# Where the operand tiles lie in SBUF: residues modulo 512 bytes in a float32r network on one core

## The chip, the cores and the metric

One core of a Trainium2 chip runs the whole program in one launch. The metric is the device time in microseconds; the median of three timed runs is 1638.51 us (1635.72, 1638.51, 1638.74). One more execution was taken with the hardware profiler, and all rows below come from it.

## The reference

A small network of 256 tokens and 1024 columns runs through ten stages, each of which adds to a residual x:

```
x = x + nsa_mixer(rms_norm(x), ...)          # sparse attention, 16 heads
x = x + swiglu(rms_norm(x), gate_up, down)   # feed forward, 2816 hidden columns
x = x + mla_mixer(rms_norm(x), ...)          # low-rank attention, 8 heads
x = x + swiglu(...)
# then, with norms before and after each part:
#   swiglu, convolution module, swiglu, swiglu, differential attention, swiglu

def swiglu(h, w_gate_up, w_down):
    gate, up = jnp.split(h @ w_gate_up, 2, axis=-1)
    return (jax.nn.silu(gate) * up) @ w_down
```

All is float32. Six of the stages are feed-forward stages of the same size; they are counted here from first to sixth.

## The kernel before

**Products.** A product of two float32 matrices is made of three float32r products, since each operand is split into a high and a low part that add up to it: low times high, high times low, high times high, into the same PSUM bank. That is `mm3` (L457 to L463), and its lines L460, L461 and L462 hold nearly all of TensorE's time. A float32r matmul has a stationary operand of 128 x 128, which TensorE loads first, and a moving operand of up to 512 columns.

**Weights.** They stream from HBM in units of 128 x 1024 (`wraw`, five buffers, SP's queue). ScalarE makes the high part (`whi`, L358, L361) and VectorE the low part (`wlo`, L359, L362), twelve buffers each. `pump` emits a piece of this work behind each product.

**A feed-forward stage** (`ffn`) multiplies x, transposed and split into `HTh` and `HTl` ([128, 2, 8, 128] each: token tile, chunk, token), by gate and up, and the hidden columns by the down weights. `ffn_order` lists its steps. There are three kinds of product:

- M, at the beginning and the end of a stage: `HT` (128 x 128) is stationary and 512 columns of weights move, into a bank `ps_g`. 192 products in a stage.
- W, in the long middle: 128 columns of weights are stationary, and both token tiles of `HT` move, as two pieces of 128 columns, 256 in all, into `ps_g`. 14 units of 48 products, 672 in a stage.
- D: the split hidden columns `hidTh` or `hidTl` (128 x 128) are stationary and 512 columns of the down weights move, into `ps_a`. 264 in a stage.

The middle is a loop of rounds: 48 W, then 12 D. The order of the instructions on TensorE is that of the program. The same kinds M and W occur in the other stages, with `HT`; the projections of the low-rank attention and the out-projection of the differential attention have other stationary operands (`ckh`, `qah`, `doTh` and their low parts) and 512 moving columns.

**Addresses.** Tiles lie in pools, and pools lie one behind the other; each tile takes its bytes per partition, rounded up to 32. Pools that are opened last (of a stage) lie last and are reused. So each address follows from the shapes of all tiles ahead of it. For the program before:

| tiles | address | modulo 512 |
|---|---|---|
| `c_g` (constants, 268 columns; holds `ident` and the gains) | 16512 | 128 |
| `ones` | 17600 | 192 |
| `x0`, `x1` | 18112, 22208 | 192 |
| `HTh`, `HTl` | 26304, 34496 | 192 |
| small pool (many tiles of some columns) | 45760 to 48895 | any |
| `wraw` x5, `whi` x12, `wlo` x12 | 48896 and on, 4096 each | 256 |
| first stage's pool for the first mixer: `c_nsa` (1 column) | 167680 | 256 |
| behind it `qT`, `kT0`, `kT1`, `V..` | 167712 and on | 288 |
| `hidTh`, `hidTl` of the 1st, 2nd, 4th and 6th feed-forward stage | 176896 and others | 256 |
| the same of the 3rd, behind `c_conv`, `hb` (16 columns), `z` | 191520 and on | 32 |
| the same of the 5th, behind `c_diff`, `lam` (4 columns), `gsub` (1) | 187712 and on | 320 |
| `doTh`, `doTl` of the differential attention | 190784, 198976 | 320 |
| `ckh`, `ckl`, `qah`, `qal` of the low-rank attention, behind `mgq` (1 column) | 192288 and on | 288 |

Of the kernel before, what the change touches and what calls it, by code (L numbers as in the profile page):

```python
# [8 lines left out]
F32 = mybir.dt.float32  # L9
# [6 lines left out]
T = 256  # L16
# [32 lines left out]
def ffn_order():  # L49
    """M: a quarter of the sums of 256 hidden columns (gate and up) of a token tile; W: gate or up of 128 hidden  # L50
    columns of both tiles, transposed; T: transpose what M made; D: 128 hidden columns into the down product;
    B: the transposes of a token tile; END: a token tile is done"""
    ops = []

    def m(t, g, hook=None):
        for q in range(4):
            if q == 2 and hook:
                ops.append(hook)
            ops.append(("M", t, g, q))

    def d(t, g, j=None):
        ops.extend(("D", t, g, i) for i in ((0, 1) if j is None else (j,)))

    m(0, 0)
    m(0, 1, ("T", 0, 0))
    d(0, 0, 0)
    ops.append(("T", 0, 1))
    d(0, 0, 1)
    d(0, 1, 0)
    ops.append(("B", 1))  # L70
    d(0, 1, 1)
    m(1, 0)
    m(1, 1, ("T", 1, 0))
    d(1, 0)
    ops.append(("T", 1, 1))
    ops.append(("W", 2, 0, 0))
    d(1, 1)
    ops.append(("W", 2, 0, 1))
    last = (2, 0)
    for g in range(2, NG - 2):  # L80
        for j in range(2):
            if (g, j) == (2, 0):
                continue
            ops.append(("W", g, j, 0))
            ops.append(("W", g, j, 1))
            d(0, *last)
            d(1, *last)
            last = (g, j)
    m(0, NG - 2)
    d(0, *last)  # L90
    d(1, *last)
    m(0, NG - 1, ("T", 0, NG - 2))
    d(0, NG - 2, 0)
    ops.append(("T", 0, NG - 1))
    d(0, NG - 2, 1)
    d(0, NG - 1)
    ops.append(("END", 0))
    m(1, NG - 2)
    m(1, NG - 1, ("T", 1, NG - 2))
    ops.append(("L", LEAD[0]))  # L100
    d(1, NG - 2, 0)
    ops.append(("T", 1, NG - 1))
    ops.append(("L", LEAD[1]))
    d(1, NG - 2, 1)
    d(1, NG - 1)
    ops.append(("END", 1))
    return ops


# ---------------------------------------------------------------- host layout  # L110
# [5 lines left out]
def lay_out(p):  # L116
    units, folds = [], {}

    def unit(a, gain=None):
        """gain: the norm gain that belongs to these rows, by name, the width of each part, and the column for each"""  # L120
        if gain:
            folds[len(units)] = gain
        a = np.ascontiguousarray(a.reshape(128, -1), dtype=np.float32)
        assert a.shape[1] <= UNIT
        units.append(a)
# [101 lines left out]
    for t in range(2):  # L227
# [5 lines left out]
        for h in range(16):  # L233
# [22 lines left out]
            ("g_sub", p["attn_subln_g_2"][0].reshape(128, 1)),  # L256
        ],
        "nsa": [
            ("live", live),
# [44 lines left out]
# ---------------------------------------------------------------- the program  # L304
class Weights:
    """The weights in the order in which they are used, each split into two float32r parts that add up to it."""
# [20 lines left out]
    def cut(self):  # L327
        """the pieces of the next unit, to be emitted one by one"""
# [22 lines left out]
    def drop(self):  # L351
        """the products with the oldest unit of the plain kind are done"""
        self.held.pop(0)
        self.refill()
# [11 lines left out]
    def room(self):  # L366
        """whether the unit that the next one takes the place of is used up"""
# [8 lines left out]
    def pump(self, n):  # L376
        """n columns of products are under way: convert a little of what comes next"""
# [27 lines left out]
class Net:  # L405
    def __init__(self, ctx, tc, io, index, widths, upto):
# [3 lines left out]
        self.small = ctx.enter_context(tc.tile_pool(name="small", bufs=3))  # L410
        self.psum = ctx.enter_context(tc.tile_pool(name="psum", bufs=1, space=bass.MemoryType.PSUM))
# [18 lines left out]
        self.nc.gpsimd.memset(self.ones, 1.0)  # L430
        self.HT = self.pair(self.main, [128, 2, 8, 128], "HT")
        self.warm(self.work(), WARM)

    def warm(self, ps, n):
        """n products that nothing uses, where the tensor engine would idle: its clock slows down if it does"""
# [29 lines left out]
    def rsqrt(self, ss, k, scale, eps, more=None, half=False, least=None, hold=True, soon=200):  # L465
        """(ss * scale + eps) ** -0.5, of k columns, halved if asked for; more: a second part of ss;
        least: 2 ** 26 eps, for each of the rows.
        Newton's steps from an estimate by the exponent, without their halves, which are put into the operand."""
# [25 lines left out]
    def split(self, hi, lo, src, scale=None):  # L494
        """hi + lo = src * scale"""
# [15 lines left out]
    def squares(self, src):  # L511
        """sums of squares along the free axis, one for each of the parts"""
# [12 lines left out]
    def ready(self, t):  # L525
        """x[t] is what the next stage starts with: start(t) transposes it into the operand of the products, and its norm
        comes after them; the gain of the norm is in the weights. norm[t]: 1 / rms, and 2 ** 26 1e-6 rms ** 2"""
# [24 lines left out]
    def preload(self, f, after):  # L552
        """the tables of a function, ahead of what needs them"""
# [3 lines left out]
    def spread(self):  # L557
        """1 / rms of all the tokens along the free axis, the same in every partition"""
# [12 lines left out]
    def lead(self, n):  # L571
        """n of the products of the first block of the next stage, for which the first token tile is ready"""
# [13 lines left out]
    def first(self):  # L586
        """the first block of a stage, and its weights"""
# [9 lines left out]
    # residual: x += scale * acc, or x += half * rms(acc) * gain  # L597
# [25 lines left out]
    # ------------------------------------------------------------ feed forward  # L623
    def ffn(self, ht, done, follow):
        nc = self.nc
        with ExitStack() as ctx:
# [11 lines left out]
            def gated(ps, t=None):  # L638
                """the gate's norm, with which the nonlinearity needs it; the other one's is left to the sums over the hidden columns"""
# [90 lines left out]
    def out_proj(self, t, oT, ws, acc=None, cs=range(8)):  # L730
        """oT [t] times a 1024 x 1024 weight, into two banks"""
# [12 lines left out]
    def own(self):  # L744
        """the next unit of the weights, and its number: out_proj marks it as used up"""
# [18 lines left out]
    # ------------------------------------------------------------ first mixer  # L764
# [5 lines left out]
    def nsa(self, ht, after):  # L770
# [3 lines left out]
        k = self.consts("nsa", keep)  # L774
        qT = keep.tile([128, 8, T], F32, name="qT", tag="qT")
        kT = [keep.tile([128, 4, T], F32, name=f"kT{b}", tag=f"kT{b}") for b in range(2)]
        V = [[keep.tile([128, 4, 64], F32, name=f"V{b}{t}", tag=f"V{b}{t}") for t in range(2)] for b in range(2)]
        gate = [keep.tile([128, 48], F32, name=f"gate{t}", tag=f"gate{t}") for t in range(2)]
        kcT = keep.tile([128, 4, 64], F32, name="kcT", tag="kcT")
        Vc = keep.tile([128, 64], F32, name="Vc", tag="Vc")  # L780
        gq = keep.tile([128, 1], F32, name="gq", tag="gq")
        inv = keep.tile([128, 2, 3], F32, name="inv", tag="inv")
# [9 lines left out]
        def operand(t):  # L792
            """x[t] as it is; its norm comes after the products"""
# [9 lines left out]
        def norms(t):  # L803
            """of the rows of x[t]: 1 / rms, half of it, and 1e-6 rms ** 2 as rsqrt takes it"""
# [42 lines left out]
        def compress(i, a):  # L847
            """a quarter of the products of both"""
# [79 lines left out]
        def block(name, t, i):  # L928
            """a quarter of a token tile times 512 columns"""
# [19 lines left out]
        gT = keep.tile([48, T], F32, name="gT", tag="gT")  # L949
# [173 lines left out]
    # ------------------------------------------------------------ second mixer  # L1123
    def tables(self, ctx):
        """the mask of the second mixer, and its rotations with the gains of its norms"""
# [10 lines left out]
    def mla(self, ht, after, tab):  # L1136
# [6 lines left out]
        gq = keep.tile([128, 1], F32, name="mgq", tag="mgq")  # L1143
# [4 lines left out]
        def rope(x, src, w, tmp):  # L1148
            """[128, n, 64]; the gains are in the tables"""
# [15 lines left out]
        # the norm of what is projected to a low rank comes after the products as well  # L1165
        rc, rc2, eq = ([self.small.tile([128, 1], F32, name=f"mv{i}{t}", tag=f"mv{i}{t}", bufs=1) for t in range(2)] for i in range(3))
# [110 lines left out]
        def attend(t, hb, bank):  # L1277
            """four heads; what it returns turns the weights, and then sums the values;
            the norm of the queries, positive, comes with the exponential"""
# [103 lines left out]
    # ------------------------------------------------------------ convolution  # L1383
    def conv_consts(self, ctx):
        pool = ctx.enter_context(self.tc.tile_pool(name="cc", bufs=1))
        k = self.consts("conv", pool)
        k["half"] = pool.tile([128, 16], F32, name="hb", tag="hb")
# [12 lines left out]
    def conv(self, k, bias_row, done):  # L1400
# [11 lines left out]
        def build(ch):  # L1412
            """four taps of 32 channels as a matrix, for each of the products of a chunk"""
# [34 lines left out]
        def spread(ch):  # L1448
            """32 channels at a time, beside themselves one, two and three tokens later"""
# [12 lines left out]
        def stats(ch, s, pc):  # L1462
            """shift is the mean of the first chunk"""
# [15 lines left out]
        def total(ch, s, sq):  # L1479
            """sums over the channels of (c - shift) and of its square"""  # L1480
# [11 lines left out]
        def weights(g, q):  # L1492
            """of 256 columns, a quarter; they have two uses"""
# [100 lines left out]
    # ------------------------------------------------------------ differential attention  # L1594
    def diff_consts(self, ctx):
# [3 lines left out]
        k["lam"] = lam = pool.tile([128, 4], F32, name="lam", tag="lam")  # L1599
# [4 lines left out]
        k["gs"] = pool.tile([128, 1], F32, name="gsub", tag="gsub")  # L1604
# [3 lines left out]
    def diff(self, k, done):  # L1608
# [113 lines left out]
        def do(kind, h, bank=None):  # L1722
            """the next step of head h; its products are followed by those of others until what they need is there"""
# [39 lines left out]
    def run(self):  # L1763
# [3 lines left out]
        def then(n, f, add=None):  # L1767
            """after a stage: the residual, and what the next stage starts with"""
# [70 lines left out]
```

## Time and profile before

| | |
|---|---|
| median of the timed runs | 1638.51 us |
| the profiled execution, first to last instruction | 1640.0 us |
| TensorE busy | 1609.4 us, 98% |
| VectorE, ScalarE busy | 1108.6 us (68%), 946.7 us (58%) |
| mean granted clock of TensorE, share of full speed | 0.992 |
| HBM read | 282.43 MB |
| W products (256 columns), whole run | 4608, recorded mean 280 to 282 ns |
| D products, whole run | 1584, recorded mean 392 to 396 ns |

A recorded duration of a matmul goes past the start of the next one, since matmuls are pipelined. What a product costs in a dense stretch is therefore read from start to start in the timeline, or from a stretch's length and its count of products. A line of the groups by shape has line, engine, operation, names out<-in, shapes, count, then the busy time in us and the mean of one in ns, then the idle time before.

### The profile page before, as it was taken

How to read it: one execution, taken by the hardware profiler on the slowest of the kernel's cores; microseconds unless marked ns; L12 is line 12 of the kernel's file. 1: busy time of each engine (PE TensorE's matmuls, PEld its weight loads, DVE VectorE, ACT ScalarE, POOL GpSimd, SP SyncE). 2: the span in 40 equal slices, each digit the busy share in tenths (PEclk: the TensorE clock that was granted, in tenths of full speed). 3: DMA queues.
4: the chain of work that ended last, by engine and by line, in shares of the span. 5: the costliest groups of instructions: out<-in, count | busy, mean ns of one | idle time of the engine just before them, and what ended most of it. 6: DMA issues, size and time to landing. Idle time of an engine off the chain costs nothing.

```text
span 1640.0 us, 27875 instructions
## 1 busy us (share of the span) xinstructions
PE 1609.4 (98%) x10351; PEld 1392.7 (85%) x10351; DVE 1108.6 (68%) x2749; ACT 946.7 (58%) x2010; POOL 33.0 (2%) x70
## 2 busy tenths in 40 slices
PE   9999999999999999999998999999999999999998
PEld 7766899887789988999886789997899889779996
DVE  6898656578856556665684585656756588796563
ACT  5788655468755445654653464545745476665451
POOL 0000100000000000000013000000000000000000
PEclk9999999999999999999999999999999999999999
DMA  6734556543455556655468175553755364256550
GB/s 237 248 121 153 189 180 197 165 158 124 153 180 180 194 167 202 224 195 187 152 198 230 26 241 182 192 192 126 243 192 185 137 224 149 65 197 223 179 173 26
DMA packets 81448, 286.48 MB, mean 175 GB/s; under 512 B 9600, under 2 KB 10368, under 8 KB 81312
## 3 DMA queue, kind: packets, MB, share of 16 engines
q1 hardware_dynamic: 75024, 269.99, 49.1%
q10 hardware_dynamic: 4288, 8.87, 1.7%
q0 software_dynamic: 2000, 5.84, 1.5%
q8 instruction: 81, 1.33, 0.3%
q14 instruction: 55, 0.45, 0.1%
HBM read 282.43 MB, written 2.23 MB: 174 GB/s over the span
## 4 chain that ended last, share of the span: by engine, by line
PE 83%; DVE 8%; DMA 4%; ACT 3%; issue 1%; POOL 0%; SPq 0%; DVEq 0%; ACTq 0%; POOLq 0%
PE ps_g L460 16%; PE ps_g L461 15%; PE ps_g L462 15%; PE ps_a L460 9%; PE ps_a L461 9%; PE ps_a L462 9%; DMA wraw<-in_stream_dram 2%; DVE wlo L362 2%; PE ps_t L1458 2%; PE ps_a L1065 1%; DMA v<-dr 1%; ACT whi L361 1%; PE ps_t L1044 1%; PE ps_g L1022 1%; ACT dS L1656 1%
## 5 line engine op out<-in xcount | busy, mean ns | idle before, releaser
L362 DVE SCALAR_TENSOR_TENSOR wlo<-wraw,c_g,whi 128x512 fp32r<-128x512 f32 (+2 forms) x689 | 481.6, 737 | 150.5 <-ACT whi L361 150.0
L361 ACT ACTIVATE whi<-wraw,c_g 128x512 fp32r<-128x512 f32 (+2 forms) x689 | 445.9, 707 | 167.6 <-PE ps_g L462 106.1
L460 PE MATMUL ps_g<-HTh,wlo 128*128 128x256 f32 (+1 forms) x1544 | 434.7, 282 | 0.3 <-DVE rs L489 0.3
L462 PE MATMUL ps_g<-HTh,whi 128*128 128x256 f32 (+1 forms) x1544 | 432.0, 280 | 0.0
L461 PE MATMUL ps_g<-HTl,whi 128*128 128x256 f32 (+1 forms) x1544 | 431.8, 280 | 0.0
L460 PEld LDWEIGHTS ps_g<-HTh,wlo 128*128 128x128 f32 (+1 forms) x1544 | 289.4, 187 | 6.7 <-issue 2.7
L462 PEld LDWEIGHTS ps_g<-HTh,whi 128*128 128x128 f32 (+1 forms) x1544 | 293.2, 190 | 0.0
L461 PEld LDWEIGHTS ps_g<-HTl,whi 128*128 128x128 f32 (+1 forms) x1544 | 289.9, 188 | 3.7 <-issue 0.4
L359 DVE TENSOR_TENSOR wlo<-wraw,whi 128x512 fp32r<-128x512 f32 x328 | 213.7, 684 | 34.3 <-ACT whi L358 34.1
L358 ACT ACTIVATE whi<-wraw 128x512 fp32r<-128x512 f32 x328 | 190.1, 623 | 51.2 <-PE ps_a L462 31.8
L460 PE MATMUL ps_g<-whi,HTl 128*128 128x512 f32 (+2 forms) x544 | 215.2, 396 | 2.1 <-ACT whi L361 1.5
L461 PE MATMUL ps_g<-wlo,HTh 128*128 128x512 f32 (+2 forms) x544 | 212.8, 391 | 1.4 <-DVE wlo L362 1.3
L462 PE MATMUL ps_g<-whi,HTh 128*128 128x512 f32 (+2 forms) x544 | 212.1, 390 | 0.0
L460 PE MATMUL ps_a<-whi,hidTl 128*128 128x512 f32 x528 | 208.2, 396 | 1.1 <-DVE hidTl L498 1.0
L461 PE MATMUL ps_a<-wlo,hidTh 128*128 128x512 f32 x528 | 207.8, 394 | 0.3 <-DVE rs L486 0.3
L462 PE MATMUL ps_a<-whi,hidTh 128*128 128x512 f32 x528 | 206.8, 392 | 0.0
L643 ACT ACTIVATE silu<-silu 128x256 f32<-128x256 f32 x84 | 34.4, 410 | 172.4 <-DVE silu L642 172.4
L460 PEld LDWEIGHTS ps_g<-whi,HTl 128*128 128x128 f32 x544 | 102.7, 189 | 25.0 <-DVE HTl L498 2.0
L461 PEld LDWEIGHTS ps_g<-wlo,HTh 128*128 128x128 f32 x544 | 102.8, 189 | 22.2 <-DVE wlo L362 2.8
L462 PEld LDWEIGHTS ps_g<-whi,HTh 128*128 128x128 f32 x544 | 102.6, 189 | 21.0
L462 PEld LDWEIGHTS ps_a<-whi,hidTh 128*128 128x128 f32 x528 | 99.2, 188 | 21.1
L460 PEld LDWEIGHTS ps_a<-whi,hidTl 128*128 128x128 f32 x528 | 98.9, 188 | 20.9 <-DVE hidTl L498 3.6
(338 smaller groups left out, 1746.6 us busy)
## 6 DMA issues: line engine op xcount, KB each, us to landing
wraw<-in_stream_dram SPq DMA_DIRECT2D x504, 512.0 KB, 4.5
v<-dr POOLq DMA_DIRECT2D x32, 142.0 KB, 7.0
rowb<-in_rows_dram ACTq DMA_DIRECT2D x7, 512.0 KB, 3.8
bias<-in_alibi_dram ACTq DMA_DIRECT2D x12, 256.0 KB, 3.4
wraw<-in_stream_dram SPq DMA_DIRECT2D x4, 384.0 KB, 3.3
wraw<-in_stream_dram SPq DMA_DIRECT2D x4, 320.0 KB, 3.4
x<-in_x_dram SPq DMA_DIRECT2D x2, 512.0 KB, 5.7
dr<-u POOLq DMA_DIRECT2D x8, 128.0 KB, 4.1
```

The source lines that it names most:

```text
L358: self.nc.scalar.activation(hi[:, s], t[:, s], AF.Copy)
L359: x = self.nc.vector.tensor_sub(lo[:, s], t[:, s], hi[:, s])
L361: self.nc.scalar.activation(hi[:, s], t[:, s], AF.Copy, scale=g)
L362: x = self.nc.vector.scalar_tensor_tensor(lo[:, s], t[:, s], g, hi[:, s], OP.mult, OP.subtract)
L460: mm(ps, ll, rh, start=first, stop=False)
L461: mm(ps, lh, rl, start=False, stop=False)
L462: mm(ps, lh, rh, start=False, stop=last)
L643: nc.scalar.activation(s, s, AF.Silu)
L1022: nc.tensor.matmul(banks[hf][:, 256 * (h // 2):256 * (h // 2) + nk], qT[64 * hf:64 * hf + 64, 2 * g + h // 2, 128 * t:128 * t + 128], kT[b ...
L1044: nc.tensor.transpose(tp[:, 128 * h:128 * h + 128], S[h][:, 128 * kb:128 * kb + 128], self.ident)
L1065: nc.tensor.matmul(ps[64 * a:64 * a + 64, 0:256], x, y.rearrange("p (i a n) -> p a i n", i=2, a=2)[:, a], start=i == 0, stop=last, tile_po ...
L1458: nc.tensor.matmul(pc[32 * r:32 * r + 32, s], W[ch][:, r, i], V[ch][:, r, 4 * i + s.start:4 * i + s.stop], start=i == 0, stop=i == 7, tile ...
```

## The change

One-column tiles move into tiles that are there already or into one new tile `cells`, some tiles are widened, and one tile `pad` is added that nothing uses. No instruction of arithmetic is added or removed, and the order in which the steps are written stays. One DMA goes: `live` becomes a column of `c_g` (269 columns now) and `c_nsa` is no more. Comments and docstrings are taken out as well. Without those, the diff is:

```diff
-            ("g_sub", p["attn_subln_g_2"][0].reshape(128, 1)),
-        ],
-        "nsa": [
-            ("live", live),
+            ("g_sub", p["attn_subln_g_2"][0].reshape(128, 1)), ("live", live),
         ],
...
         self.small = ctx.enter_context(tc.tile_pool(name="small", bufs=3))
+        self.small.tile([128, 32], F32, name="pad", tag="pad", bufs=1)
...
         self.nc.gpsimd.memset(self.ones, 1.0)
+        self.cells = self.const.tile([128, 16], F32, name="cells", tag="cells")
...
-        k = self.consts("nsa", keep)
+        k = {"live": c["live"]}
...
+        kcT = keep.tile([128, 4, 64], F32, name="kcT", tag="kcT")
+        gT = keep.tile([48, T], F32, name="gT", tag="gT")
+        Vc = keep.tile([128, 64], F32, name="Vc", tag="Vc")
         gate = [keep.tile([128, 48], F32, name=f"gate{t}", tag=f"gate{t}") for t in range(2)]
-        kcT = keep.tile([128, 4, 64], F32, name="kcT", tag="kcT")
-        Vc = keep.tile([128, 64], F32, name="Vc", tag="Vc")
         gq = keep.tile([128, 1], F32, name="gq", tag="gq")
-        inv = keep.tile([128, 2, 3], F32, name="inv", tag="inv")
+        inv = keep.tile([128, 88], F32, name="inv", tag="inv")[:, 0:6].rearrange("p (t i) -> p t i", t=2)
...
-        gT = keep.tile([48, T], F32, name="gT", tag="gT")
...
-        gq = keep.tile([128, 1], F32, name="mgq", tag="mgq")
+        gq = self.cells[:, 0:1]
...
-        rc, rc2, eq = ([self.small.tile([128, 1], F32, name=f"mv{i}{t}", tag=f"mv{i}{t}", bufs=1) for t in range(2)] for i in range(3))
+        rc, rc2, eq = ([self.cells[:, 1 + 2 * i + t:2 + 2 * i + t] for t in range(2)] for i in range(3))
...
-        k["half"] = pool.tile([128, 16], F32, name="hb", tag="hb")
+        k["half"] = pool.tile([128, 72], F32, name="hb", tag="hb")[:, 0:16]
...
-        k["lam"] = lam = pool.tile([128, 4], F32, name="lam", tag="lam")
+        k["lam"] = lam = self.cells[:, 8:12]
...
-        k["gs"] = pool.tile([128, 1], F32, name="gsub", tag="gsub")
+        k["gs"] = self.cells[:, 12:13]
```

By the same rule as above, all tiles of the table from `x0` on lie at 256 modulo 512 in the program after, the small pool apart; `wraw`, `whi` and `wlo` keep their addresses.

## Rows read from the trace of the kernel before

**Rows 1.** The page: busy time and share of each engine; the chain.

```profile
PE 1609.4 (98%) x10351; PEld 1392.7 (85%) x10351; DVE 1108.6 (68%) x2749; ACT 946.7 (58%) x2010; POOL 33.0 (2%) x70
...
PE 83%; DVE 8%; DMA 4%; ACT 3%; issue 1%; POOL 0%; SPq 0%; DVEq 0%; ACTq 0%; POOLq 0%
```

**Rows 2.** Busy us of each engine (instructions), clock, DMA: four stretches, eleven rounds each.

```profile
214.95:307.00 92.05, 92.05 (x661) 86.94 (x660) 55.76 (x100) 46.19 (x86) 0.00 (x0) 1.00 0.60 195
684.55:775.10 90.55, 90.55 (x661) 84.67 (x660) 55.78 (x100) 46.20 (x86) 0.00 (x0) 1.00 0.59 199
1186.25:1278.00 91.75, 91.75 (x661) 85.87 (x660) 55.57 (x100) 46.12 (x86) 0.00 (x0) 1.00 0.59 196
1494.85:1586.85 92.00, 92.00 (x661) 86.89 (x660) 55.78 (x100) 46.18 (x86) 0.00 (x0) 1.00 0.58 196
```

**Rows 3.** By shape, first stage, 214.95 to 307.00: count, busy us, mean ns, idle.

```profile
L460 PE MATMUL ps_g<-HTh,wlo 128*128 128x256 f32 x176 | 49.5, 281 | 0.0
...
L461 PE MATMUL ps_a<-wlo,hidTh 128*128 128x512 f32 x44 | 17.1, 389 | 0.0
```

**Rows 4.** The same, third stage, 684.55 to 775.10.

```profile
L460 PE MATMUL ps_g<-HTh,wlo 128*128 128x256 f32 x176 | 48.6, 276 | 0.0
...
L461 PE MATMUL ps_a<-wlo,hidTh 128*128 128x512 f32 x44 | 17.4, 396 | 0.0
```

**Rows 5.** The same, fifth stage, 1186.25 to 1278.00.

```profile
L460 PE MATMUL ps_g<-HTh,wlo 128*128 128x256 f32 x176 | 49.1, 279 | 0.0
...
L461 PE MATMUL ps_a<-wlo,hidTh 128*128 128x512 f32 x44 | 17.4, 395 | 0.0
```

**Rows 6.** Timeline, first stage: start us, length us, engine, line; 48, then 12 products.

```profile
223.29 0.28 PE L460 MATMUL ps_g<-HTh,wlo 128*128 128x256 f32 x1
...
228.95 0.39 PE L460 MATMUL ps_a<-whi,hidTl 128*128 128x512 f32 x1
...
231.67 0.28 PE L460 MATMUL ps_g<-HTh,wlo 128*128 128x256 f32 x1
```

**Rows 7.** Timeline, third stage, at the same places.

```profile
684.54 0.28 PE L460 MATMUL ps_g<-HTh,wlo 128*128 128x256 f32 x1
...
689.99 0.39 PE L460 MATMUL ps_a<-whi,hidTl 128*128 128x512 f32 x1
...
692.78 0.28 PE L460 MATMUL ps_g<-HTh,wlo 128*128 128x256 f32 x1
```

**Rows 8.** Timeline, HT stationary: first stage (24 between), before the fifth (35 between).

```profile
315.40 0.39 PE L460 MATMUL ps_g<-whi,HTl 128*128 128x512 f32 x1
...
320.89 0.39 PE L460 MATMUL ps_a<-whi,hidTl 128*128 128x512 f32 x1
...
1154.71 0.40 PE L460 MATMUL ps_g<-whi,HTl 128*128 128x512 f32 x1
...
1162.87 0.39 PE L462 MATMUL ps_g<-whi,HTh 128*128 128x512 f32 x1
```

**Rows 9.** Groups by shape, convolution (850 to 900), then differential attention (1348 to 1412).

```profile
L462 PE MATMUL ps_g<-HTh,whi 128*128 128x256 f32 x62 | 17.5, 282 | 0.0
...
L461 PE MATMUL ps_g<-HTl,whi 128*128 128x256 f32 x127 | 35.3, 278 | 0.0
```

**Rows 10.** Stretches as in rows 2: around the convolution, and the differential attention.

```profile
800.00:960.00 160.00, 149.72 (x1341) 120.66 (x1340) 109.59 (x269) 80.73 (x174) 22.64 (x40) 0.97 0.51 152
...
1300.00:1470.00 170.00, 166.14 (x998) 141.37 (x997) 138.48 (x463) 113.75 (x273) 0.00 (x0) 0.99 0.43 143
```

**Rows 11.** Timeline, first stage, after two transposes: eight products of 512 columns between.

```profile
331.18 0.40 PE L461 MATMUL ps_a<-wlo,hidTh 128*128 128x512 f32 x1
...
333.00 0.39 PE L460 MATMUL ps_a<-whi,hidTl 128*128 128x512 f32 x1
```

**Rows 12.** Timeline, first microseconds: ScalarE's first arithmetic, and what it waited for.

```profile
4.76 0.63 ACT L517 ACTIVATE junk<-x 128x512 f32<-128x512 f32 x1 [1.82 <-DMA x<-in_x_dram]
```

**Rows 13.** A reader of the small mv tiles: count, ns min/median/max, when, shape.

```profile
L1309 ACT ACTIVATE mPT<-ps_t,mv x6: 681/688/710, 404.6 to 433.2; 128x512 f32<-128x512 f32 x6
```

## The prediction, as written before the result was known

> **What bounds the kernel now.** The page comes first: TensorE is busy 98% of the 1640.0 us, VectorE 68%, ScalarE 58%, and the chain of work that ended last runs through TensorE for 83% of the span [rows 1]. A busy TensorE alone proves little, since the ends of matmuls are modelled, so the next view is a table of stretches from the steady middle of four of the six feed-forward stages. In each the 661 matmuls leave no gap (92.05 us busy of 92.05 in the first), while VectorE needs 55.8 us, ScalarE 46.2 us, and the DMA engines are 0.6 busy [rows 2]. There the time is the number of products times the distance from the start of one to the start of the next, and nothing else.
>
> What the reader is to see in that table is that the same eleven rounds of the same loop take 92.05 us in the first stage and 92.00 in the sixth, but 90.55 in the third and 91.75 in the fifth. The instructions, shapes and order are the same; the weights differ in value only. Grouped by shape, the stretches show where it comes from: in the first stage a 256-column product is recorded with 281 ns and a 512-column one with 389 [rows 3]; in the third with 276 and 396 [rows 4]; in the fifth with 279 and 395 [rows 5]. The recorded duration holds a constant for the pipeline, so I take distances from start times. First stage: 48 products of 256 columns from 223.29 to 228.95 us are 117.9 ns each, 12 of 512 columns from 228.95 to 231.67 are 226.7 [rows 6]. Third stage: 684.54 to 689.99 is 113.5, 689.99 to 692.78 is 232.5 [rows 7]. The other kind of 512-column product, HT stationary and weights moving, takes (320.89 - 315.40) / 24 = 228.8 ns in the first stage and (1162.87 - 1154.71) / 35 = 233.1 before the fifth [rows 8].
>
> What differs between these stages is where the tiles lie, which follows from the shapes (the table in the section on the kernel). The weights are at 256 modulo 512 everywhere, HT at 192. The hidden operand is at 256 in the first, second, fourth and sixth stage, at 32 in the third and at 320 in the fifth. So equal residues of the two operands give 226.7 ns; residues 64 apart give 228.8 to 233.1; 32 against 256 gives 232.5. For the 256-column products both operands have the same residues (192 moving, 256 stationary) in all stages, yet they run at 113.5 or at 117.9; which of the two they fall into depends on what ran before them. 226.7 is twice 113.35: the equal-residue product and the faster of the two modes have the same cost per column, which I read as a product without a stall. The others stall 2 to 6 ns each.
>
> **The change part by part.** All addresses below are worked out from the shapes.
>
> Moving HT. `cells` (64 bytes) stands ahead of x0 in the constant pool, so x0 goes from 18112 to 18176, and HTh from 26304 to 26368: residue 256. The six [128,1] tiles that leave the small pool (192 bytes) and the pad (128) make up for it, so the weights stay where they are.
>
> (a) 256-column products of the feed-forward stages: 14 units of 48, 672 in a stage. If equal residues do for them what they do for the 512-column ones, all run at 113.5. The first, second, fourth and sixth stage (the second and fourth by residue, the sixth also by its 92.00 us) get 672 x 4.4 ns = 2.96 us shorter each, 11.8 together. In the fifth the mean of 279 lies midway between 281 and 276, so half of its products gain: 336 x 4.4 = 1.5. The third has it already. No row shows a 256-column product with equal residues. The bounds are 0 gained with the third stage falling back to 117.9, and the whole; I take the whole, since the nearest row is the 512-column product with equal residues, whose weight load meets the moving operand in the same way.
>
> (b) The products into the down projection, 264 in a stage, in the third and fifth: 2 x 264 x (232.5 - 226.7) = 3.1 us. Both ends are rows: 226.7 is what the first stage does.
>
> (c) HT stationary: 192 a stage, 1152 in six: x (228.8 - 226.7) = 2.4 us, and 36 at 233.1 in the fifth add 0.1: 2.5 us. Here moving 256 and stationary 256 is just what (b) shows.
>
> (d) Outside the feed-forward stages: the other 720 of kind (c), 1.5 us by the same difference; 198 products with operands at 320 or 288 (out-projection of the differential attention, low-rank projections), at 6 ns 1.2 us; and the 256-column products of the convolution and the differential attention, some 184 at a mean of 282 and some 380 at 278 against 276 [rows 9], 1.1 + 0.8 us. These 4.6 us lie where TensorE waits for others (149.72 busy of 160 in the stretch with the convolution, 166.14 of 170 with the differential attention [rows 10]), so a faster product is partly a longer wait. I count half, 2.3 us.
>
> (e) Settling. After an interruption even equal residues need some products: 331.18 to 333.00 us, right after two transposes, is 227.5 ns over 8 [rows 11]. 0.8 ns on some 1,300 products costs 1.0 us of what (b) to (d) promise.
>
> The rest costs nothing that I can find. `live` joins `c_g`, so one small DMA goes from ScalarE's queue; ScalarE's first arithmetic waits until 4.76 us for x, which SP's queue brings, so nothing on the path moves [rows 12]. The columns of `cells` replace one-column tiles. If the order were kept by tile rather than by column, each of the 14 small VectorE instructions on them could wait for a ScalarE reader of up to 0.7 us [rows 13], 10 us at the very most; the columns don't overlap, so I take 0. The other moved tiles keep shapes and users. Nothing new can become the bound: a round of the third stage's 256-column products and the first's 512-column ones is 48 x 113.5 + 12 x 226.7 = 8.17 us, against VectorE's 55.8 / 11 = 5.07 and ScalarE's 4.20.
>
> Sum: 11.8 + 1.5 + 3.1 + 2.5 + 2.3 - 1.0 = 20.2 us. Against the profiled execution 1640.0 - 20.2 = 1619.8. The median of the three timed runs, 1638.51, is 1.5 below that execution, so I forecast 1618 us.
>
> **The rivals.**
>
> No effect of addresses. The same product would cost the same wherever its operands lie, and the differences between stages would come from the data or from what ran before. For it: the 256-column product has two speeds at one pair of residues. Against it: the stage at residue 256 has 389 ns and the two at other residues 396 and 395. It gives 1638 us. The Trainium skill, "TensorE: Matmul & The Clock Gate", section on what happens when a matmul is issued, says that TensorE reads its moving operand and its weights through two independent ports, so that loading the next weights takes no read bandwidth from the running product; "SBUF — State Buffer", section "Who interferes with whom", adds that TensorE and ScalarE never wait on anyone. By these rules the change is worth nothing; the 6 ns between stages in this trace speaks against them.
>
> The 256-column products stay at 117.9. Then (b) and (c), half of the 1.5 and 1.2 in (d), and (e) give 3.1 + 2.5 + 1.35 - 1.0 = 6.0 us; the third stage falls back from 113.5 (672 x 4.4 = 3.0) and the fifth too (1.5). Net 1.5 us: 1637, no change. For it: at 117.9 the mode that they enter from equal-residue products is stable through whole stages, and the third stage enters its fast mode from products that the change takes away. Against: that mode was seen only with residues 64 apart.
>
> Between the two: some stretches lock and some don't, as in the fifth stage now: about 1628.
>
> Slower: in these products the stationary operand is a weight slice of 512 bytes and the moving one two pieces of 512 bytes of HT; once all start at the same residue they could meet on every product. The price by the worst steady row: 233.1 - 226.7 = 6.4 over 113.5, 119.9 ns. That costs 4 x 672 x 2.0 = 5.4, third stage 672 x 6.4 = 4.3, fifth 336 x 8.4 = 2.8, outside 0.8: 13.3, less the 6.0: +7.3, so 1646. It decides from a distance above 118.0 (today's mean over the six stages is 116.8; 6.0 us over 4608 products is 1.3 ns). Against it: equal residues are the fastest case wherever the trace has them.
>
> **How the numbers follow.** Forecast 1618, chance 0.62, own range 1613 to 1625: the lower end counts (d) whole and (e) at nothing and gives back some of the clock in the convolution (0.97 granted between 800 and 960 us, 1.00 in the rounds [rows 2, 10]), the upper takes away (d) and half a stage or two of (a). Mixed 0.08, no locking 0.14, no effect 0.06, slower 0.10. A measurement of this kernel tells about 0.2%, 3.3 us, from no change: faster means below 1635.2. Faster gets the forecast, the mixed case and a little of no locking: 0.72. Within 0.2%: 0.17. Slower: 0.11. The range reaches from 1613 to 1639 and leaves out the slower rival and the edges.
>
> **What would show it.** In the profile after, the grouped 256-column products at 276 in all six feed-forward stages (the forecast) or 281 (no locking) or above 282 (slower); the 512-column ones at 389 in the third and fifth stage too; HT-stationary stretches at 226.7 by start times; the eleven rounds at 90.55 - 0.8 = 89.8 us in each stage. The prediction is wrong if those rounds fall to 89.8 and the span doesn't follow, which would need a wait that this trace doesn't show, or if the 256-column mean is above 279.

## The result, and the profile after

The changed kernel takes 1648.06 us (median of five runs, 1643.87 to 1650.86) against 1638.51: ratio 1.0054, 95% interval 1.0036 to 1.0071. The forecast was 1618; what came is the rival "slower", which gave 1646. The profiled execution went from 1640.0 to 1649.1 us, at a granted clock of 0.995 (0.992 before). TensorE stays the bound [rows 1]; this is its line of the page after:

```profile
PE 1616.8 (98%) x10351; PEld 1404.5 (85%) x10351; DVE 1107.9 (67%) x2749; ACT 945.4 (57%) x2010; POOL 32.9 (2%) x70
```

The table of stretches answers [rows 2]. Here each stretch holds eleven whole rounds, from the start of one group of W products to the start of another: first, third, fifth and sixth feed-forward stage of the kernel after.

```profile
213.60:307.10 93.50, 93.50 (x661) 88.09 (x660) 55.73 (x100) 46.14 (x86) 0.00 (x0) 1.00 0.58 193
...
686.54:780.04 93.50, 93.50 (x661) 88.10 (x660) 55.73 (x100) 46.17 (x86) 0.00 (x0) 1.00 0.58 192
...
1193.54:1287.04 93.50, 93.50 (x661) 88.10 (x660) 55.72 (x100) 46.16 (x86) 0.00 (x0) 1.00 0.58 193
1502.42:1595.92 93.50, 93.50 (x661) 88.09 (x660) 55.73 (x100) 46.14 (x86) 0.00 (x0) 1.00 0.58 192
```

The same cut in the kernel before, first, third and fifth stage (the stretches of [rows 2] ended 0.06 to 0.24 us short of eleven rounds):

```profile
214.91:307.02 92.11, 92.11 (x661) 86.96 (x660) 55.80 (x100) 46.23 (x86) 0.00 (x0) 1.00 0.60 196
...
684.53:775.24 90.71, 90.71 (x661) 84.79 (x660) 55.80 (x100) 46.22 (x86) 0.00 (x0) 1.00 0.59 199
...
1186.14:1278.13 91.99, 91.99 (x661) 86.06 (x660) 55.81 (x100) 46.23 (x86) 0.00 (x0) 1.00 0.59 195
```

The change did make the stages alike: all six now take the same 93.50 us. But that is above the slowest of before, and all of it is TensorE without a gap, while VectorE and ScalarE work as before. Grouped by shape, first stage, and behind the "..." third stage (answering [rows 3, 4]; each line number is one lower than before):

```profile
L459 PE MATMUL ps_g<-HTh,wlo 128*128 128x256 f32 x176 | 49.7, 283 | 0.0
...
L460 PE MATMUL ps_a<-wlo,hidTh 128*128 128x512 f32 x44 | 17.3, 392 | 0.0
...
L459 PE MATMUL ps_g<-HTh,wlo 128*128 128x256 f32 x176 | 49.7, 283 | 0.0
...
L460 PE MATMUL ps_a<-wlo,hidTh 128*128 128x512 f32 x44 | 17.3, 392 | 0.0
```

283 for the 256-column products is the mark that the prediction had set for "slower" (above 282). The distances come from the timeline of the first stage: the first W of a round, its first D, the first W of the next round; then the first of 24 M and the D behind them (answering [rows 6, 8]).

```profile
213.61 0.28 PE L459 MATMUL ps_g<-HTh,wlo 128*128 128x256 f32 x1
...
219.36 0.40 PE L459 MATMUL ps_a<-whi,hidTl 128*128 128x512 f32 x1
...
222.11 0.28 PE L459 MATMUL ps_g<-HTh,wlo 128*128 128x256 f32 x1
...
315.61 0.39 PE L459 MATMUL ps_g<-whi,HTl 128*128 128x512 f32 x1
...
321.05 0.39 PE L459 MATMUL ps_a<-whi,hidTl 128*128 128x512 f32 x1
```

W: (219.36 - 213.61) / 48 = 119.8 ns (117.9 and 113.5 before). D: (222.11 - 219.36) / 12 = 229 ns (226.7 and 232.5 before); the single starts show 233, 236, 228, 233, 231 and then 226 to 227, so the first five after a group of W are late. In the first stage of the kernel before, all twelve came at 226 to 227. M: (321.05 - 315.61) / 24 = 226.7 ns (228.8 before).

Over whole groups the unrounded starts give W 119.85 ns (117.8, in the third stage 113.6 before) and D 228.9 to 229.0 (226.7, in the third 232.8). So W is 4 x 672 x 2.1 + 672 x 6.2 + 672 x 4.1 = 12.6 us dearer (the last term is the fifth stage, where groups at 113.8 and at 117.9 took turns, 115.8 on average). D loses 4 x 168 x 2.3 = 1.5 us in four stages and gains 2 x (168 x 3.8 + 96 x 5.8) = 2.4 in the third and fifth. M gains about the forecast 2.5. Together +9.2 us; the spans differ by 9.1. So close a match is partly chance: the sum leaves out the W outside the six stages, some 2 us dearer too, and five executions of the changed kernel spread over 7 us.

### The profile page after: what moved, and what is told of

The parts are those of the page before. It is cut to its first block, busy times and chain, and to the rows that moved or that the text cites. A ratio compares the mean times of both kernels' runs of the same rounds, so it can differ in the third digit from the quotient of the medians.

```text
span 1649.1 us, 27872 instructions
## 1 busy us (share of the span) xinstructions
PE 1616.8 (98%) x10351; PEld 1404.5 (85%) x10351; DVE 1107.9 (67%) x2749; ACT 945.4 (57%) x2010; POOL 32.9 (2%) x70
## 5 line engine op out<-in xcount | busy, mean ns | idle before, releaser
L459 PE MATMUL ps_g<-HTh,wlo 128*128 128x256 f32 (+1 forms) x1544 | 439.3, 285 | 0.9 <-DVE rs L488 0.9
L461 PE MATMUL ps_g<-HTh,whi 128*128 128x256 f32 (+1 forms) x1544 | 437.1, 283 | 0.0
L460 PE MATMUL ps_g<-HTl,whi 128*128 128x256 f32 (+1 forms) x1544 | 436.9, 283 | 0.0
L459 PEld LDWEIGHTS ps_g<-HTh,wlo 128*128 128x128 f32 (+1 forms) x1544 | 295.3, 191 | 7.1 <-issue 2.7
L460 PEld LDWEIGHTS ps_g<-HTl,whi 128*128 128x128 f32 (+1 forms) x1544 | 295.4, 191 | 3.5 <-issue 0.4
```

The costliest lines, as they stand in the source:

```text
L459: mm(ps, ll, rh, start=first, stop=False)
L460: mm(ps, lh, rl, start=False, stop=False)
L461: mm(ps, lh, rh, start=False, stop=last)
```

## The experiments

Theory: with the residue of HT made equal to that of the weights, every 256-column product stalls by 119.9 - 113.3 = 6.6 ns. Rival: the loss comes with the merged tiles or the moved pools, not with HT.

**Undoing the move of HT alone.** `cells` goes behind HT, so HT and x are at 192 again (x is no operand of W, D or M); all else stays as changed.

```diff
-        self.cells = self.const.tile([128, 16], F32, name="cells", tag="cells")
         self.HT = self.pair(self.main, [128, 2, 8, 128], "HT")
+        self.cells = self.main.tile([128, 16], F32, name="cells", tag="cells")
```

> The changed kernel with x and HT back at 192 modulo 512; the stage pools stay at 256. Theory (HT's move costs the time): the 256-column products go back from 120 to 117.9 or 113.5 ns, HT-stationary ones to 228.8, those into the down projection are 226.7 in all six stages. Against the kernel before, the third stage takes 3.0 us more (its 256-column products now come from equal residues, 117.9) and 1.5 less (down), the fifth 1.5 more and 1.6 less, the other parts 0.6 less: about 1639, ratio 1.000 to 1.002. Rival (the one-column tiles in one tile, or the stage pools, cost it): it stays at 1648, ratio 1.005.

1639.34 us against 1638.94 for the kernel before on the same chip, ratio 0.9999 (0.9986 to 1.0012). Eleven rounds in the first, second and third stage:

```profile
212.69:304.80 92.11, 92.11 (x661) 86.97 (x660) 55.79 (x100) 46.23 (x86) 0.00 (x0) 1.00 0.59 195
494.77:586.88 92.11, 92.11 (x661) 86.97 (x660) 55.78 (x100) 46.22 (x86) 0.00 (x0) 1.00 0.60 196
682.06:774.17 92.11, 92.11 (x661) 86.96 (x660) 55.77 (x100) 46.19 (x86) 0.00 (x0) 1.00 0.59 196
```

The whole loss is gone with HT's move. The third stage is the point to see: its hidden operand is now at the weights' residue, its D fell to 226.7, and its W rose from 113.6 to 117.8, as in the other stages. The moved pools and merged tiles together, without HT's move, are worth nothing net that can be measured.

**Moving HT alone.** The stage pools get back the residues of before (32 and 320 for the hidden operand of the third and fifth stage, 288 for the low-rank tiles); HT stays at 256.

```diff
+        keep.tile([128, 1], F32, name="shift1", tag="shift1")
...
-        gq = self.cells[:, 0:1]
+        gq = keep.tile([128, 1], F32, name="mgq", tag="mgq")
...
-        k["half"] = pool.tile([128, 72], F32, name="hb", tag="hb")[:, 0:16]
+        k["half"] = pool.tile([128, 16], F32, name="hb", tag="hb")
...
-        k["lam"] = lam = self.cells[:, 8:12]
+        k["lam"] = lam = pool.tile([128, 4], F32, name="lam", tag="lam")
...
-        k["gs"] = self.cells[:, 12:13]
+        k["gs"] = pool.tile([128, 1], F32, name="gsub", tag="gsub")
```

> HT moves to 256 alone: the pools of the stages keep the residues of the kernel before (hidden operand at 32 in the third feed-forward stage, 320 in the fifth, others 288 and 320). Theory: 256-column products at 120 ns in all six stages, HT-stationary ones at 226.7, those into the down projection 232 to 233 in the third and fifth stage. That is 1648 plus 2 x 264 x 3.6 ns = 1650, ratio 1.006 to 1.008. Rival (the stage pools cost it): 1638, ratio 1.000.

1649.29 us, ratio 1.0061 (1.0045 to 1.0076). First and third stage:

```profile
212.34:305.84 93.50, 93.50 (x661) 88.10 (x660) 55.72 (x100) 46.13 (x86) 0.00 (x0) 1.00 0.58 192
...
685.58:779.45 93.87, 93.87 (x661) 87.96 (x660) 55.69 (x100) 46.10 (x86) 0.00 (x0) 1.00 0.58 192
```

W is at 119.5 to 119.9 in all six stages, behind D products at 228.9 to 233.8: with equal residues no fast mode showed behind any of them. Both runs bear the theory out and leave nothing for the rival.

**The price of each difference, by itself.** The network is left out; groups of 48 products of 256 columns (or 36 of 512) of the same three-product scheme run on constant tiles, each group at another residue, behind 512-column products with equal residues or 32 bytes apart.

```python
for e in (0, 32):
    for m in range(0, 512, 32):
        down(4, e)        # 12 of 512 columns, stationary e bytes off
        trans(m, 0, 2)    # 48 of 256 columns in two pieces, moving m bytes off
...
for s in range(0, 512, 32):
    down(4, 0)
    down(12, s)           # 36 of 512 columns, stationary s bytes off
```

> This kernel leaves out the whole network: it copies x to the output and between that runs nothing but products, 48 of 256 columns (two pieces of 128, as HT is read) at a time, for 16 residues of the moving operand in steps of 32 bytes against a stationary operand at 256, each behind 12 products of 512 columns whose operands have equal residues, and a second time behind 12 whose residues differ by 32; then the same with one piece of 256 columns, with other stationary residues, and 12 products of 512 columns at 16 residues of the stationary operand. Theory (the difference of the two residues sets the distance): 120 ns at a difference of 0, 113.3 to 118 at moving 64 below stationary, where what ran before decides between the two; and other differences give one of 113 to 120, the same for a given difference whatever the two residues are. Rival 1 (the place of HT, not the difference): all 16 residues alike. Rival 2 (what ran before alone): all residues alike behind equal products, and all alike, at another value, behind the others.

Distances in ns, each the mean of the last 24 inside a group. The table repeats after 256 bytes, not 512, in every column; "off" is moving minus stationary for 256 columns and stationary minus moving for 512 (HT, or the hidden operand, minus weights in both).

| bytes off, modulo 256 | 0 | 32 | 64 | 96 | 128 | 160 | 192 | 224 |
|---|---|---|---|---|---|---|---|---|
| 256 columns, behind equal residues | 120.0 | 116.7 | 117.8 | 120.0 | 120.0 | 118.6 | 117.8 | 118.3 |
| 256 columns, behind 32 off | 120.0 | 116.7 | 117.8 | 120.0 | 118.8 | 118.6 | 113.3 | 118.3 |
| 512 columns | 226.7 | 233.3 | 233.3 | 234.2 | 232.1 | 233.3 | 228.9 | 233.3 |

Seven groups of it in a table of stretches (length, TensorE busy, count, clock). The count includes the product still running at the start. 256 columns: 0 off, 32 off, 192 off, 192 off behind unequal products (48 each); 512 columns: 32 off, 192 off (36 each), 0 off (60, less the cut at the start).

```profile
94.20:99.94 5.74, 5.74 (x49) 1.00 0.00 0
102.70:108.29 5.59, 5.59 (x49) 1.00 0.00 0
144.95:150.59 5.64, 5.64 (x49) 1.00 0.00 0
280.35:285.81 5.46, 5.46 (x49) 1.00 0.01 3
434.65:443.03 8.38, 8.38 (x37) 1.00 0.00 0
490.34:498.57 8.23, 8.23 (x37) 1.00 0.00 0
509.75:523.30 13.55, 13.55 (x61) 1.00 0.00 1
```

These are the prices of the network: 192 off behind equal D (first stage before), 192 off behind unequal D (third stage before), 0 off (after). Zero is the best for 512 columns and, with 96 and 128, the worst for 256. What ran before matters at 192 off and, by 1.2 ns, at 128. With the stationary operand moved instead, in steps of 64, the distances followed the difference again (117.8 at 64 and 192 off, 120.0 at 0 and 128), so the difference counts and not the place of HT. One piece of 256 columns in place of two gave the same at 0, 64, 128 and 192 off, so the two pieces are not the cause.

**Unequal hidden operand in all stages.** If D sets W's mode, then giving all six stages what the third had before must make W fast everywhere: HT at 192, hidden operand at 32. The edit comes on top of the one that undid the move of HT.

```diff
             pool = ctx.enter_context(self.tc.tile_pool(name="ffn", bufs=3))
+            pool.tile([128, 72], F32, name="shift", tag="shift", bufs=1)
```

> The changed kernel with x and HT at residue 192 again, and the hidden operand at residue 32 in all six FFN stages (the third had that before). Theory: the 256-column products run at 113.4 to 113.5 ns in all six stages (117.8 before in four of them), the 512-column ones with the hidden operand at 232.6 (226.7 before in four). Per stage 672 x 4.4 ns = 2.96 us gained and 264 x 5.9 ns = 1.56 us lost, 1.4 us a stage, some 6 to 8 us in all: 1631 to 1633 us, ratio 0.995 to 0.997. Rival: the third stage's 113.5 ns came from something else than the hidden operand's residue (its tiles' other places, or its surroundings); then the 256-column products stay at 117.8 and only the loss is left: 1639 + 9 = 1648 us.

1632.81 us against 1639.66, ratio 0.9951 (0.9933 to 0.9970). First, second and third stage:

```profile
214.05:304.76 90.71, 90.71 (x661) 84.79 (x660) 55.80 (x100) 46.22 (x86) 0.00 (x0) 1.00 0.61 199
494.82:585.54 90.72, 90.72 (x661) 84.78 (x660) 55.80 (x100) 46.23 (x86) 0.00 (x0) 1.00 0.61 199
681.09:771.80 90.71, 90.71 (x661) 84.79 (x660) 55.79 (x100) 46.23 (x86) 0.00 (x0) 1.00 0.60 199
```

W runs at 113.6 in every stage although D pays 232.8. This is the opposite of the change, for the operand of D, and it is faster than both kernels.

**Which products set the mode.** The network left out, rounds of 48 W at 192 off and 12 D at mixed offsets:

```python
plans = [[u] * 4 for u in range(0, 256, 32)]                 # three products for each entry
plans += [[0, 0, u, u] for u in (32, 64, 192)]
plans += [[u, u, 0, 0] for u in (32, 192)]
plans += [[0, 0, 0, u] for u in (32, 192)]
plans += [[(0, 32)] * 4, [(32, 0)] * 4, [(0, 192)] * 4]      # high and low part apart
```

> A microbenchmark that leaves the network out: rounds of 48 products of 256 columns (moving 192 bytes off the stationary one, the pair that took 117.7 ns behind 512-column products of equal residue and 113.35 ns behind ones 32 bytes off) and 12 products of 512 columns, three rounds for each choice of the offsets of the 512-column ones. Theory: what goes before sets the mode of the 256-column group, whatever the offset, as long as it is not 0 or 128: 113.35 ns behind offsets 32, 64, 96, 160, 192 and 224, 117.8 ns behind 0; behind mixed groups the last products decide, so six equal products followed by six unequal ones give 113.35, the other order 117.8. Rival: the mode needs a whole group of unequal products, and every mixture with equal ones gives 117.8. Second rival: the mode hangs on the distance 32 alone. The offset 192 should cost 229.1 ns for each 512-column product, against 232 to 234 for the others and 226.7 for 0.

Half of this missed. Which products came last mattered: six equal and then six at 32 give 113.5, nine equal and then three at 32 give 113.9, six at 32 and then six equal give 117.8. But the offset matters, against my expectation: with all twelve at 160 both groups behind them took 113.5 to 114.0, at 96, 192 and 224 both took 117.8, and at 32, 64 and 128 one of two identical rounds was fast and the other not (in the fifth stage before, with the hidden operand 64 off, fast and slow groups took turns as well). High and low part apart gave 117.8 for (0, 32) and 113.4 to 113.9 for (32, 0) and (0, 192). Three groups of 48 W: behind 12 equal D, behind 6 equal and 6 at 32, behind 6 equal and 6 at 64:

```profile
269.10:274.74 5.64, 5.64 (x49) 5.64 (x48) 0.00 (x0) 0.00 (x0) 1.00 0.00 0
...
249.92:255.36 5.44, 5.44 (x49) 5.44 (x48) 0.00 (x0) 0.00 (x0) 1.00 0.02 3
277.51:283.15 5.64, 5.64 (x49) 5.64 (x48) 0.00 (x0) 0.00 (x0) 1.00 0.00 0
```

At 192 off the product has two steady states, and the last products ahead of the group have a part in the choice. As identical rounds came out both ways, offsets alone don't settle it; that the alignment in time does is a guess that no run here tests.

**Two offsets in one product, and which reads meet.** The network left out again. In groups of 48 W behind equal D the two pieces of the moving operand lie at different residues: the first m bytes off the weights, the second d bytes further. A first part alternates two kinds of product, so that the next stationary operand lies x bytes off the running moving one while a product's own operands lie elsewhere.

```python
w = 1024 + d // 4
r = [h[:, o:o + 2 * w].rearrange("p (t n) -> p t n", t=2)[:, :, 0:128] for h in (hh, hl)]
...
s, m = ((64 + x, 0), (x, 64))[c % 2]    # stationary, moving, in turn
```

> A microbenchmark that leaves the network out, on which reads meet. First part: products of two kinds in turn, the moving operand at 0 and at 64 bytes, so placed that the next product's stationary operand lies x bytes off the moving one that streams meanwhile, while a product's own stationary and moving operands are 64 bytes more or less apart; x from 0 to 224, with 256 and with 512 columns. If the stall is between the next weight load and the running stream, 256 columns give 120.0 ns at x 0 and 119.9 at x 128, and 512 columns 226.7 at x 0; rival, a product's own two operands matter: x 0 then gives what offsets of 64 and 192 gave, 117.8 for 256 columns and 229 to 234 for 512, and the least of 512 columns falls at 64 or 192. Second part: groups of 48 products of 256 columns whose two pieces are d bytes apart in residue, the first m bytes off the stationary operand, behind equal 512-column products: with d 0 the table as measured (0: 120.0, 32: 116.7, 64: 117.8, 96: 120.2, 128: 119.9, 160: 118.5, 192: 117.8, 224: 118.3). If the two pieces stall each by its own offset, the other entries lie between those of m and m + d, none under 116.5; rival: the change of offset inside a product breaks the stall, and some pair gets to 113.3 behind equal products, which the kernel could use.

On which reads meet both theories fell: at x = 0, 256 columns took 119.9 ns, as the first had it, but 512 columns took 231.7 and not 226.7; the least of 512 columns is 230.0, at 96, 128 and 224, where neither puts it. Of the 64 pairs of offsets one reached 113.3 behind equal products, m = 64 with d = 192: pieces 64 and 0 bytes off. Neither of these offsets alone is under 117.8. That group, and one at m = 192 with d = 192 that took 120.0:

```profile
545.96:551.40 5.44, 5.44 (x49) 5.44 (x48) 0.00 (x0) 0.00 (x0) 1.00 0.00 0
579.32:585.07 5.75, 5.75 (x49) 5.75 (x48) 0.00 (x0) 0.00 (x0) 1.00 0.00 0
```

**That pair in the kernel.** One tile for both parts of HT, padded between the token tiles; the hidden operand stays at the weights' residue, as the change has it. `cells` goes behind HT here too. To make room, the pad and three spare buffers of small tiles go, and two small tiles of the low-rank attention share `R`.

```diff
-        self.HT = self.pair(self.main, [128, 2, 8, 128], "HT")
+        self.main.tile([128, 32], F32, name="gap", tag="gap")
+        both = self.main.tile([128, 2, 2096], F32R, name="HT", tag="HT")
+        self.HT = [both[:, :, 1024 * i:1024 * i + 1024].rearrange("p t (c n) -> p t c n", c=8) for i in range(2)]
```

> The changed kernel with the high and low parts of HT in one tile, laid out so that its first token tile lies 64 bytes and its second one 0 bytes (modulo 256) off the weights; the hidden operand stays at the weights' residue. In the microbenchmark that pair of offsets alone took the 256-column products to 113.3 ns behind equal 512-column products. Theory (the microbenchmark carries over): W 113.5 in all six stages, products with hidden operand about 228.5 behind each group and 226.7 later, those with HT 233.5 in token tile 0 and 226.7 in token tile 1. Against the kernel with HT at 192 and the hidden operand at 32 (1632.8): 936 x 4.1 ns and 648 x 5.5 ns gained, 1872 x 1 ns lost: 1627 us, ratio 0.991 to 0.994. Rival: in the kernel's surroundings the pair falls to another mode, 117 to 120 ns for each product of 256 columns; then 4032 x 4 to 6 ns come on top: 1642 to 1651. Second rival: one tile for both parts adds waits between the engines that write it, and the time lies above 1633 with every product as fast as forecast.

1629.04 us against 1639.07, ratio 0.9948 (0.9930 to 0.9965). First and third stage:

```profile
214.51:304.71 90.20, 90.20 (x661) 84.79 (x660) 55.85 (x100) 46.26 (x87) 0.00 (x0) 1.00 0.60 200
...
679.87:770.07 90.20, 90.20 (x661) 84.79 (x660) 55.84 (x100) 46.27 (x87) 0.00 (x0) 1.00 0.61 200
```

The products came close to the forecast, W 113.7, D 228.7, M in groups without a gap 233.4 in token tile 0 and 226.9 in token tile 1; the time lies 2 us above it.

**The two side by side**, the same kernels on one chip:

> The kernel with HT at residue 192 and the hidden operand at 32 once more, now side by side with the one whose two pieces of HT lie 64 and 0 bytes off. Its rounds took 90.71 us for eleven against 90.20, its profiled span 1632.2 against 1627.2 us. If the rest of the program costs the same in both: 1632 to 1634 here. Rival: the gap of 3.8 us between the medians of separate runs came from the chip or the time of the run; then both medians lie within 1 us.

> The kernel with the two token tiles of HT 64 and 0 bytes off the weights, side by side with the one above: 0.51 us less in eleven rounds makes about 3.6 us over six stages of 13 rounds, and the other products with the hidden operand (227 against 233 ns) some 3 us, less 1 to 2 us for those with HT: 1627 to 1630 us, 3 to 5 us below the other. Rival: within 1 us of it.

1632.39 us (ratio 0.9954, 0.9933 to 0.9976) and 1627.59 us (0.9935, 0.9919 to 0.9951): 4.8 us apart, as expected from the products. The second is the fastest version here, 11.4 us under the kernel before and some 20 under the changed one.

One group matters here, since it corrects a reading of [rows 8]. Ahead of the fifth stage stand 36 M, with the stationary operand 192 off. The kernel with the hidden operand at 32 ran on two chips; this is that group in the profiled execution on the first, then on the second:

```profile
1148.25:1156.66 8.41, 8.41 (x37) 1.00 0.65 207
...
1147.23:1155.49 8.26, 8.26 (x37) 1.00 0.62 198
```

The single starts give 233.3 ns in the one and 229.3 in the other. In the first execution the like groups of 36 ahead of the first three stages took 229.0 to 229.3. So at 192 off 512-column products have two steady distances too, and the operands' addresses alone don't choose.

## Why the prediction was wrong

**What bounds the kernel** was right: dense stretches of TensorE whose length is products times distance. That the distance hangs on residues was right too; the medians of these kernels, whose arithmetic is the same and whose tiles lie elsewhere, run from 1627.6 to 1649.3 us.

**(a) failed, and with it the forecast.** The step was: "the nearest row is the 512-column product with equal residues, whose weight load meets the moving operand in the same way". It does not. The same pair of residues gives the 512-column product its best distance (226.7) and the 256-column product one of its worst (120.0). Forecast at 113.5, W ran at 119.85: in place of 13.3 us less it took 12.6 more, 26 of the 29 us between the forecast and the result. The bounds taken for (a) went no higher than 117.9, though no row showed the case. The clue was in the trace: 113.5 came at residues 64 apart, so for this shape a product without a stall did not need equal ones.

**(b) half right.** The third and fifth stage gained, but to 229 and not 226.7 behind each group of W; and the four stages that had 226.7 lost 1.5 us, which the sum did not have. This follows from (a): behind W at 192 off and 117.8 ns, D ran at 226.7 from the first product, so the late start came with the new distance of W, and (e) had put settling down to interruptions only.

**(c) right** in its sum: 226.7 for HT stationary, about 2.5 us. But its 233.1 before the fifth stage is not fixed by the addresses of the operands; it is the slower of two distances at 192 off. **(d)** went with (a): in the differential attention the recorded means rose from 278 to 283 [rows 9], and W outside the six stages lost some 2 us in place of the forecast gain. **The edits at nothing** cost nothing: with HT moved back they measure 0.9999.

**The rivals.** "Slower" had the direction and the price, 119.9 ns. That the price fits to 0.1 ns is luck: it was borrowed from a 512-column product at other residues, the slower of its two distances. It got 0.10, on the argument that equal residues are the fastest case wherever the trace has them; all those rows were of 512 columns. "No effect of addresses" fell: moving HT alone costs 0.6%. The rule of the Trainium skill that weighed for it ("TensorE: Matmul & The Clock Gate", the section on what happens when a matmul is issued: weights and moving operand come through independent ports) does not cover these distances, 113.3 to 120.0 ns for one shape on the same engine at clock 1.00. "No locking" was right that the third stage's fast mode came from the D products that the change took away; the run with HT at 192 shows just that, at 0.9999; but W did not stay at 117.9.

What stays open: which two reads meet, why 192 off has two states and what chooses between them, and why 64 with 0 breaks the stall.

## What to carry to other kernels

Where one engine runs without a gap, read the distance from start to start for each shape and stage before a cause is named; one shape's best placement says nothing for another. A case that no row shows needs a bound on both sides of zero, and a table of it (64 cases cost one run here) is cheaper than the argument. Change one operand's place at a time: here the same move made one shape 2 ns faster and the other 2 to 6 ns slower.

## What was not expected of the hardware

- A float32r product of 256 columns takes 113.3 to 120.0 ns and one of 512 columns 226.7 to 234.2, by the difference of its operands' SBUF addresses modulo 256 bytes and, at some differences, by what ran before.
- Equal addresses modulo 256 are best for 512 columns and among the worst for 256.
- At 192 bytes off, 256-column products have two steady distances, 113.3 and 117.8, and keep for 48 products the one they entered with. 512-column products have two as well, 228.9 and 233.3.
- After a group of 256-column products at 0 off, equal 512-column products take about five of 228 to 236 ns to settle at 226.7; after a group at 192 off and 117.8 ns they take none.
- A moving operand in two pieces at 64 and 0 bytes off reaches 113.3 behind equal products, though one offset throughout gives 117.8 and 120.0.
